# A decoder block in split fp32: VectorE and ScalarE keep the traced order from the big sets on, and the operands of w_down's parts are made at other places

## Chip, cores, metric

The kernel runs on one core of a Trainium2 chip. The metric is the device time of one execution in microseconds. Before the change it is 2761.99 us, the median of 3 runs (2760.24 to 2762.66).

## The reference

One decoder block over 512 tokens, model width 2048, in float32: two token mixers (latent attention and a gated DeltaNet) merged by gates, then a SwiGLU channel mixer of width 5632. The change lies in the channel mixer:

```python
h = _rmsnorm(x, norm_ffn[l]) * (1.0 + sc_f) + sh_f
gate, up = jnp.split(h @ w_gate_up[l], 2, axis=-1)
x = x + gt_f * ((jax.nn.silu(gate) * up) @ w_down[l])
...
return _rmsnorm(x, final_norm)
```

## The kernel before

**Split products.** Every float32 operand is split into a high part (a cast on ScalarE) and a low part (a subtraction on VectorE), and a product is three matmuls: high by high, low by high, high by low. Weights are read from HBM by loads on SP into tiles named `raw` or `raws`, split into `hi` and `lo`, and used by TensorE; four buffers hold each of `hi` and `lo`. Activations are kept as pairs too (`hilo`, L239 the cast and L240 the subtraction). All helpers of TensorE are recorded at L155.

**The driver.** The kernel's work is a list of units (L47 to L115). A unit has a load, a split, matmuls, and code before and after them. `fill` keeps `deep` units split ahead of the one that runs, and `ahead` more loaded (`LOADS`, or 2 where a unit sets it). While matmuls are traced, every `GROUP` = 12 of them the driver makes one `pump`: each side chain (a generator) goes one step further. `yield n` lets a chain rest for n pumps. So the Python code fixes a traced order: which evictions, splits and side steps stand between which matmuls.

**What sets the order on an engine.** `Core` wraps the engines in `PINNED`, before the change SP, GpSimd and TensorE, with `Ordered`: their instructions are carried out in the traced order. VectorE and ScalarE were not wrapped: there the tile layer's scheduler chose an order of its own.

**The channel mixer's stages.** `gu0` and `gu_both(1)` make the first columns of gate and up. `big(s)`, s = 1 to 10, makes 512 columns of each as a Strassen-like set of 7 products: 16 units, the first eight with 24 matmuls of 512 columns, the last eight with 18. `sums` (L1701) makes sums of weight blocks, `split` (L1722, L1723) their halves; the eviction code `after` (L1740 and on) combines the products from PSUM with VectorE, some with ScalarE, and `activated` multiplies silu(gate) by up later. The activations go to DRAM (`f_dram`), or stay as `aT`.

Then w_down. `dn(36, n)`, four plain sets of 2 units with 24 matmuls each; `strassen_down(0, n)`, n = 0 to 3, Strassen-like sets over 2048 rows of w_down; `dn(40, n)`; `strassen_down(1, n)`, whose last set runs in `last_dn` with the closing norm. A set of `strassen_down` has 8 units of 42 matmuls of 256 columns. Each unit's split has three sums (L1889), two casts (L1897) and two subtractions (L1898), of 768 and 1024 columns. The last unit of a set evicts: a copy of the first product (L1916, ScalarE), then seven sums on VectorE (L1913). Outputs are scaled on ScalarE (L1857) and added to DRAM by GpSimd.

**The operands of `strassen_down`.** `sums_down(ks)` is a side chain that makes the activations' combinations for q = 0 to 3; units 2q and 2q + 1 of each set use those of q. For each q it loads four blocks `a11`, `a21`, `a22`, `a12` from `f_dram` (`fetch_a`), makes four combinations (L1998) and splits seven operands with `hilo`, in four pumps of 3, 3, 3 and 2 VectorE instructions. `free(q)` says from when q may be made; it counts the operands of the earlier half that are done with (`gone`). While q is made, the next q's loads can be started step by step through `next(fetching, None)`. `down_ready` forces the remaining steps if a unit needs an operand that is not made yet. `dn` and `last_dn` use `wlh`, splits of w_down and of weights in another form, also by `hilo`.

Of the kernel before, what the change touches and what calls it, by code (L numbers as in the profile page):

```python
# [34 lines left out]
class Unit:  # L35


    def __init__(self, load=None, split=None, mms=None, pre=None, post=None, weight=1, alone=False, late=False):
        self.load = load
        self.split = split  # L40
        self.mms = mms
        self.pre = pre
        self.post = post
        self.weight = weight
        self.alone = alone
        self.late = late
# [97 lines left out]
class Ordered:  # L144


    def __init__(self, tc, engine):
        self.tc = tc
        self.engine = engine

    def __getattr__(self, name):
        f = getattr(self.engine, name)

        def call(*args, **kwargs):
            return self.tc.keep_in_program_order(f(*args, **kwargs))  # L155

        return call


class Core:  # L160
    def __init__(self, tc, pinned):
        nc = tc.nc
        for e in ("tensor", "vector", "scalar", "gpsimd", "sync"):
            setattr(self, e, Ordered(tc, getattr(nc, e)) if e in pinned else getattr(nc, e))

# [4 lines left out]
def block_kernel(ctx: ExitStack, tc: tile.TileContext, a: dict, out, out_t):  # L172
    nc = Core(tc, PINNED)
    drv = Driver()
# [372 lines left out]
    def logits_done(first):  # L547
        def done(ps):
            for j, q in enumerate(ps):
# [6 lines left out]
                        ks=[(k, 1) for k in range(KT)])  # L556
# [900 lines left out]
    def with_pre(units, fn):  # L1457
        u = units[0]
        p0 = u.pre

        def pre():
            fn()
            if p0 is not None:
                p0()
        u.pre = pre
        return units
# [177 lines left out]
    def combine():  # L1644

        for q in range(4):
            while h2n[1] < 2 * q + 10:
                yield
            a11, a12, a21, a22 = h2f[0][q], h2f[0][q + 4], h2f[1][q], h2f[1][q + 4]
            res = {}  # L1650
            for name, x, y, op in (("x5", a22, a21, ALU.subtract), ("x6", a11, "x5", ALU.add), ("x7", a11, a21, ALU.subtract),
                                   ("x3", "x6", a12, ALU.subtract)):
                x, y = (res.get(v, v) if isinstance(v, str) else v for v in (x, y))
                s = res[name] = S(name)
                nc.vector.tensor_tensor(s[:], x[:], y[:], op)
            comb[q] = {}
            for name in ("x3", "x6", "x7", "x5"):
                comb[q][name] = hilo(res.pop(name)[:], name)
                yield 2
            for h in range(2):  # L1660
                h2f[h][q] = h2f[h][q + 4] = None
            xn[0] = q + 1
# [304 lines left out]
    def sums_down(ks):  # L1967

        ahead = []

        def free(q):
            return q < 4 and gone[ks] >= min(q + 2, 4) and (q < 3 or plain_sets[0] > 4 * ks + 3)

        def fetch_a(q):
            v = {}
            for name, i, h in (("a11", 8 * ks + q, 0), ("a21", 8 * ks + q, 1), ("a22", 8 * ks + 4 + q, 1), ("a12", 8 * ks + 4 + q, 0)):
                v[name] = S(name)
                load(v[name][:], f_dram[i, h])
                yield 2
            ahead.append(v)  # L1980

        for q in range(4):
            if not ahead:
                yield from until(lambda: free(q))
                yield from fetch_a(q)
                yield 5
            v = ahead.pop(0)
            more = free(q + 1)
            if more:
                fetching = fetch_a(q + 1)  # L1990
            v["x7"] = S("x7")
            d = {}
            for c, dst, x, y, op in (("m7", "x7", "a11", "a21", ALU.subtract), ("m1", "a11", None, None, None),
                                     ("m5", "a21", "a22", "a21", ALU.subtract), ("m4", "a22", None, None, None),
                                     ("m6", "a11", "a11", "a21", ALU.add), ("m2", "a12", None, None, None),
                                     ("m3", "a12", "a11", "a12", ALU.subtract)):
                if op is not None:
                    nc.vector.tensor_tensor(v[dst][:], v[x][:], v[y][:], op)  # L1998
                d[c] = hilo(v[dst][:], "x")
                if op is None:  # L2000
                    if more and next(fetching, None) is None:
                        more = False
                    yield
            v = None
            if more:
                yield from fetching
            down[ks][q] = d
            made[ks] = q + 1
            yield
# [24 lines left out]
    def gu_both(s):  # L2034

        st = {}

        def unit(k0):
            box = {}

            def start():
                box["raw"] = fetch(gu_loads(s)(k0, 2), 512, 2)

            def split():
                box["w"] = halves(box.pop("raw"), 512, 2)

            def pre():
                if k0 == 0:
                    st["ps"] = [PS(f"gu{s}") for _ in range(4)]
                    st["done"] = gu_done(s, st["ps"])  # L2050

            def after(j, h):
                st["done"](j, h)

            mms = []
            for kk in range(2):
                k = k0 + kk
                for j in range(4):
                    for h in range(2):
                        for n, (wi, xi) in enumerate(((0, 0), (0, 1), (1, 0))):  # L2060
                            mms.append(lambda kk=kk, k=k, j=j, h=h, n=n, wi=wi, xi=xi: mm(
                                st["ps"][j][:, 256 * h:256 * h + 256], box["w"][wi][:, kk, tok(j)], half_k(h2T[h][k // 2], k)[xi],
                                start=k == 0 and h == 0 and n == 0, stop=k == KT - 1 and n == 2, skip_group_check=True))
                        if k == KT - 1:
                            mms[-1] = lambda m=mms[-1], j=j, h=h: (m(), after(j, h))

            def post():
                if k0 + 2 == KT:
                    for q in range(4):
                        h2T[1][q] = None  # L2070

            return Unit(start, split, mms, pre, post, late=k0 + 2 == KT)

        return [unit(k0) for k0 in range(0, KT, 2)]
# [15 lines left out]
    xc = []  # L2090

    def ffn():
        def gu0():
            us, st = [], {}

            def done(ps):
                done_ = gu_done(0, ps)
                for j in range(4):
                    for h in range(2):
                        done_(j, h)  # L2100

            for h in range(2):
                half = fm_set("gu0", gu_loads(0), 512, KT, lambda k, h=h: half_k(h2T[h][k // 2], k), done if h else None, st=st,
                              cols=slice(256 * h, 256 * h + 256), alone=True)
                for i, u in enumerate(half):
                    def ahead(h=h, k=min(2 * i + 4, KT)):
                        while h2n[h] < k:
                            drv.step(h2c[h])
                    with_pre([u], ahead)
                us.append(half)  # L2110

            def start():
                for j in range(KT):
                    mixT[j] = None
                start_h2(1)()
            with_pre(us[0], start)
            return us[0] + us[1]
# [171 lines left out]
        def finished(segs):  # L2289
# [3 lines left out]
            for q in range(8):  # L2293
# [3 lines left out]
                if q % 2:  # L2297
                    yield

        yield from gu0()  # L2300
        yield from with_pre(gu_both(1), lambda: xc.append(drv.add(combine())))
        assert known == {4, 5}
        side(g_dram.rearrange("(k p) -> p k", p=P), gt_ffn[:])
        nc.vector.tensor_scalar(gt_neg[:], gt_ffn[:], -1.0, None, op0=ALU.mult)
        euvw.append(wides.tile([P, 4, 512], F32, tag="wide", name="euvw"))
        for s in range(1, 11):
            for i, u in enumerate(big(s)):
                if (s, i) == (10, 10):
                    with_pre([u], lambda: maker.__setitem__(0, drv.add(sums_down(0))))
                yield u  # L2310

# [1 line left out]
            drv.ahead = LOADS  # L2313
        for n in range(4):
            for k, u in enumerate(dn(36, n)):
                yield with_pre([u], more)[0]
                if n in (1, 2):
                    yield Unit(mms=turned_a(2 * n + k - 2), pre=lambda: drv.finish(chains["act"]))
        for n in range(4):
# [7 lines left out]
                yield u  # L2327
        for n in range(4):
            for u in dn(40, n):
                yield with_pre([u], more)[0]  # L2330
        for n in range(3):
            yield from strassen_down(1, n)
        yield from last_dn()
# [62 lines left out]
```

## Time and profile before

| | us |
|---|---|
| median of 3 runs | 2761.99 |
| the profiled execution | 2757.97 |
| its span in the trace | 2755.9 |
| of it, the big sets | 1484.20 to 2264.36 |
| `dn(36)` | 2264.36 to 2309.80 |
| `strassen_down(0, 0)` begins | 2309.64 |
| `strassen_down(1, 0)` begins | 2527.07 |

A page of the profile gives busy time by engine; PE is TensorE, DVE VectorE, ACT ScalarE, POOL GpSimd, SP the engine that issues most loads. Because TensorE is almost always busy, its few idle places matter, and its granted clock, which is 1.00 at full speed. In a list of waits, "PE m <- DVE xl" is idle time of TensorE before a matmul into m that ended when VectorE had written xl.

### The profile page before, as it was taken

The numbers are of one execution on the slowest core, as the hardware profiler recorded it, in microseconds if no ns is written. First come the engines' busy times: TensorE is split into PE (matmuls) and PEld (weight loads), VectorE is DVE, ScalarE is ACT, GpSimd is POOL, SyncE is SP. The second block draws the span as 40 slices with busy tenths as digits, with TensorE's granted clock in tenths as the row PEclk, the third lists the DMA queues.
The fourth block names the chain that finished last, engine by engine and source line by source line (L and its number), as shares of the span: only waits on it lengthen the run. The fifth ranks groups of instructions, "written<-read, shape, count | busy, mean of one in ns | idle before, by whom it ended". The sixth has DMA issues, their size and how long they took to land.

```text
span 2755.9 us, 39855 instructions
## 1 busy us (share of the span) xinstructions
PE 2726.4 (99%) x14896; PEld 2348.2 (85%) x14896; DVE 2017.6 (73%) x3193; ACT 1168.9 (42%) x1649; POOL 251.5 (9%) x334
## 2 busy tenths in 40 slices
PE   9999999999999999999999999999999999999998
PEld 7888788888888888888999888888888888998997
DVE  8884657676967547785487877778877867878876
ACT  3443432542344343222373444444444445446545
POOL 0000011102100000001000000000000103113113
PEclk9999999999999999999999999999999999999999
DMA  9996556546754648885464565666565668469565
GB/s 350 313 364 203 152 162 179 190 146 182 211 150 153 203 143 287 306 298 195 158 182 146 189 202 199 207 213 201 200 210 191 213 204 193 115 194 207 123 190 173
DMA packets 308538, 557.93 MB, mean 202 GB/s; under 512 B 39956, under 2 KB 109748, under 8 KB 308216
## 3 DMA queue, kind: packets, MB, share of 16 engines
q1 hardware_dynamic: 259848, 461.09, 51.6%
q0 software_dynamic: 28704, 66.37, 9.3%
q10 hardware_dynamic: 19792, 27.92, 2.9%
q8 instruction: 116, 1.90, 0.3%
q14 instruction: 78, 0.64, 0.1%
HBM read 474.52 MB, written 80.76 MB: 201 GB/s over the span
## 4 chain that ended last, share of the span: by engine, by line
PE 94%; DVE 2%; DMA 2%; issue 1%; ACT 1%; SPq 0%; ACTq 0%; DVEq 0%; POOLq 0%
PE m L155 37%; PE wo L155 6%; PE gb L155 6%; PE v L155 4%; PE gu L155 3%; PE z L155 3%; PE ga L155 3%; PE ya L155 3%; PE k L155 3%; PE dn L155 3%; PE q L155 3%; PE yb L155 3%; PE s L155 3%; PE ckv L155 2%; PE cq L155 2%; PE qk L155 1%
## 5 line engine op out<-in xcount | busy, mean ns | idle before, releaser
L263 ACT CAST hi<-raw 128x1024 fp32r<-128x1024 f32 (+1 forms) x274 | 285.2, 1042 | 666.7 <-DMA raw<-in_w_in_dram 131.2
L264 DVE TENSOR_TENSOR lo<-raw,hi 128x1024 fp32r<-128x1024 f32 (+1 forms) x274 | 337.2, 1232 | 305.4 <-ACT hi L263 291.8
L1722 ACT CAST hi<-raws 128x512 fp32r<-128x512 f32 (+1 forms) x240 | 218.4, 910 | 329.0 <-PE m L155 270.4
L1723 DVE TENSOR_TENSOR lo<-raws,hi 128x512 fp32r<-128x512 f32 (+1 forms) x240 | 247.7, 1044 | 86.5 <-ACT hi L1722 86.3
L155 PE MATMUL m<-xl,hi 128*128 128x256 f32 x896 | 257.1, 287 | 3.8 <-DVE xl L240 3.8
L155 PE MATMUL m<-xh,hi 128*128 128x256 f32 x896 | 256.8, 287 | 3.7 <-ACT xh L239 2.3
L155 PE MATMUL m<-xh,lo 128*128 128x256 f32 x896 | 256.6, 286 | 0.8 <-DVE lo L1898 0.8
L435 DVE CUSTOM_DVE_ANT_0 rawm<-rawm,cbc 128x1024 f32<-128x1024 f32 x192 | 234.1, 1238 | 7.8 <-DMA rawm<-in_w_mod_dram 7.2
L155 PE MATMUL m<-hi,h2h 128*128 128x512 f32 x480 | 190.7, 397 | 0.4 <-DVE euvw L1740 0.3
L155 PE MATMUL m<-hi,h2l 128*128 128x512 f32 x480 | 187.2, 390 | 0.0
L155 PE MATMUL m<-lo,h2h 128*128 128x512 f32 x480 | 186.8, 389 | 0.0
L155 PEld LDWEIGHTS m<-xl,hi 128*128 128x128 f32 x896 | 175.0, 195 | 4.7 <-DVE xl L240 4.7
L155 PEld LDWEIGHTS m<-xh,hi 128*128 128x128 f32 x896 | 175.0, 195 | 4.4 <-ACT xh L239 2.7
L155 PEld LDWEIGHTS m<-xh,lo 128*128 128x128 f32 x896 | 175.2, 196 | 1.0 <-DVE lo L1898 1.0
L1722 ACT CAST hi<-sums 128x1024 fp32r<-128x1024 f32 x80 | 84.2, 1052 | 109.2 <-PE m L155 104.2
L1723 DVE TENSOR_TENSOR lo<-sums,hi 128x1024 fp32r<-128x1024 f32 x80 | 97.8, 1222 | 27.3 <-ACT hi L1722 26.8
L155 PE MATMUL wo<-mh,hi 128*128 128x512 f32 (+1 forms) x320 | 111.2, 347 | 0.0
L155 PE MATMUL wo<-mh,lo 128*128 128x512 f32 (+1 forms) x320 | 110.9, 347 | 0.0
L155 PE MATMUL wo<-ml,hi 128*128 128x512 f32 (+1 forms) x320 | 110.9, 347 | 0.0
L1897 ACT CAST hi<-sums 128x1024 fp32r<-128x1024 f32 x64 | 67.1, 1048 | 99.0 <-PE m L155 76.7
L1898 DVE TENSOR_TENSOR lo<-sums,hi 128x1024 fp32r<-128x1024 f32 x64 | 78.2, 1223 | 39.8 <-ACT hi L1897 39.6
L155 PEld LDWEIGHTS m<-hi,h2l 128*128 128x128 f32 x480 | 90.1, 188 | 19.5
(535 smaller groups left out, 7315.9 us busy)
## 6 DMA issues: line engine op xcount, KB each, us to landing
raws<-in_w_gate_up_dram SPq DMA_DIRECT2D x400, 256.0 KB, 3.5
rawm<-in_w_mod_dram SPq DMA_DIRECT2D x192, 512.0 KB, 5.5
raw<-in_w_in_dram SPq DMA_DIRECT2D x144, 512.0 KB, 4.7
raws<-in_w_down_dram SPq DMA_DIRECT2D x128, 256.0 KB, 4.1
raw<-in_w_o_dram SPq DMA_DIRECT2D x40, 512.0 KB, 4.6
s_dram<-raws POOLq DMA_DIRECT2D x80, 256.0 KB, 2.3
raws<-s_dram SPq DMA_DIRECT2D x80, 256.0 KB, 3.3
rawa<-in_w_in_dram SPq DMA_DIRECT2D x32, 512.0 KB, 4.4
```

The lines of the kernel that those rows point to most:

```text
L155: return self.tc.keep_in_program_order(f(*args, **kwargs))
L263: nc.scalar.copy(hi[:], raw[:])
L264: (lo_eng or nc.vector).tensor_tensor(lo[:], raw[:], hi[:].bitcast(F32), ALU.subtract)
L435: r = nc.vector.tensor_tensor_reduce(raw, raw, c, 1.0, 0.0, ALU.mult, ALU.add, parts[:, k, half:half + 1])
L1722: nc.scalar.copy(hi[:], src)
L1723: nc.vector.tensor_tensor(lo[:], src, hi[:].bitcast(F32), ALU.subtract)
L1897: nc.scalar.copy(hi[:], src)
L1898: nc.vector.tensor_tensor(lo[:], src, hi[:].bitcast(F32), ALU.subtract)
```

## The change

From the first of the big sets on, VectorE and ScalarE keep the traced order too: all five engines are wrapped, and `on` of those two is set there. `free` gets lower thresholds, `fetch_a` and the pause after it yield fewer pumps, and `sums_down(0)` starts two units earlier. The loads go two units ahead rather than four from unit 3 of `gu_both(1)` on and from the third set of each `dn`.

```diff
@@ class Ordered
-    def __init__(self, tc, engine):
+    def __init__(self, tc, engine, on=True):
         self.tc = tc
         self.engine = engine
+        self.on = on
...
-            return self.tc.keep_in_program_order(f(*args, **kwargs))
+            ins = f(*args, **kwargs)
+            return self.tc.keep_in_program_order(ins) if self.on else ins
@@ class Core
-            setattr(self, e, Ordered(tc, getattr(nc, e)) if e in pinned else getattr(nc, e))
+            setattr(self, e, Ordered(tc, getattr(nc, e), e in pinned))
@@ def sums_down(ks)
-            return q < 4 and gone[ks] >= min(q + 2, 4) and (q < 3 or plain_sets[0] > 4 * ks + 3)
+            return q < 4 and gone[ks] >= (0 if ks == 0 else 2, 2, 3, 4)[q] and (q < 3 or plain_sets[0] > 4 * ks + 3)
...
                 load(v[name][:], f_dram[i, h])
-                yield 2
+                yield
...
                 yield from fetch_a(q)
-                yield 5
+                yield 3
@@ the channel mixer
+        def few():
+            drv.ahead = 2
+
         yield from gu0()
-        yield from with_pre(gu_both(1), lambda: xc.append(drv.add(combine())))
+        us = with_pre(gu_both(1), lambda: xc.append(drv.add(combine())))
+        with_pre([us[3]], few)
+        yield from us
...
+        nc.vector.on = nc.scalar.on = True
         for s in range(1, 11):
             for i, u in enumerate(big(s)):
-                if (s, i) == (10, 10):
+                if (s, i) == (10, 8):
                     with_pre([u], lambda: maker.__setitem__(0, drv.add(sums_down(0))))
                 yield u
...
             for k, u in enumerate(dn(36, n)):
-                yield with_pre([u], more)[0]
+                yield with_pre([u], more if n < 2 else few)[0]
...
             for u in dn(40, n):
-                yield with_pre([u], more)[0]
+                yield with_pre([u], more if n < 2 else few)[0]
```

Traced this way, the first loads and steps of q land at other places: q0 of half 0 is made in units 12 to 15 of the tenth big set (before, in `dn(36)`), q1 in `dn(36)` (before, at the start of the first `strassen_down` set), q0 of half 1 in unit 6 of `strassen_down(0, 3)` (before, in `dn(40)`). The order of TensorE's and GpSimd's instructions is the same in both kernels. SP issues 38 loads from `f_dram` in place of 32.

## The prediction

> **What bounds the kernel now.** First the page:
>
> ```profile
> span 2755.9 us, 39855 instructions
> PE 2726.4 (99%) x14896; PEld 2348.2 (85%) x14896; DVE 2017.6 (73%) x3193; ACT 1168.9 (42%) x1649; POOL 251.5 (9%) x334
> ```
>
> TensorE works 99% of the span. The change removes no instruction from it, so it can gain only where TensorE waits or runs at a lower clock. Where that is, the table of windows shows (window, its length, then busy time and instructions of PE, weight loads, DVE, ACT and POOL, granted clock, DMA share, GB/s):
>
> ```profile
> 1484.20:2264.36 780.16, 779.80 (x3508) 644.95 (x3507) 609.00 (x701) 349.82 (x417) 62.82 (x116) 1.00 0.61 202
> 2264.36:2309.80 45.44, 45.44 (x211) 37.60 (x210) 28.26 (x41) 24.15 (x38) 20.34 (x21) 1.00 0.93 207
> 2309.80:2353.75 43.95, 37.88 (x277) 36.59 (x276) 40.62 (x65) 23.78 (x35) 3.87 (x4) 0.89 0.57 157
> 2485.30:2530.00 44.70, 44.70 (x210) 37.50 (x210) 32.46 (x48) 30.57 (x49) 20.48 (x19) 1.00 1.05 226
> 2530.00:2573.00 43.00, 43.00 (x360) 43.00 (x360) 41.65 (x66) 24.02 (x35) 3.87 (x6) 1.00 0.52 126
> 2661.00:2705.00 44.00, 41.83 (x334) 41.41 (x333) 28.81 (x46) 21.50 (x39) 8.97 (x14) 0.96 0.74 232
> ```
>
> In order: the big sets (0.36 us idle in 780), `dn(36)` (none), `strassen_down(0,0)` (6.07 us idle, clock 0.89), `dn(40)` (none), `strassen_down(1,0)` (none, though VectorE is busy 41.65 of 43) and `strassen_down(1,3)` (2.17 us idle). The waits of TensorE from 1400 on (us, times, longest) name the same places:
>
> ```profile
> PE m L155 <- DVE xl L240: 3.8, 4, 1.2
> PE m L155 <- ACT xh L239: 2.3, 2, 1.1
> PE m L155 <- ACT hi L1897: 1.4, 1, 1.4
> PE m L155 <- DVE lo L1898: 0.8, 1, 0.8
> PE m L155 <- DVE euvw L1740: 0.3, 1, 0.3
> ```
>
> The first two are the operands that `sums_down` makes, late in `strassen_down(0,0)`; the next two are the weight split in `strassen_down(1,3)`. An idle stretch also costs clock behind it, as 5-us windows around the stretches show:
>
> ```profile
> 2330.00:2335.00 5.00, 2.23 (x13) 1.53 (x11) 5.00 (x9) 1.92 (x3) 0.00 (x0) 0.85 0.07 25
> 2335.00:2340.00 5.00, 4.48 (x21) 4.48 (x22) 4.40 (x9) 2.39 (x4) 0.00 (x0) 0.50 0.31 102
> 2350.00:2355.00 5.00, 4.04 (x18) 3.84 (x19) 4.11 (x8) 0.83 (x1) 0.00 (x0) 0.56 0.29 90
> 2355.00:2360.00 5.00, 5.00 (x35) 5.00 (x34) 1.25 (x2) 1.73 (x3) 0.00 (x0) 0.76 0.36 105
> 2675.00:2680.00 5.00, 2.83 (x16) 2.42 (x15) 4.26 (x6) 2.71 (x4) 0.00 (x0) 0.83 0.58 193
> 2680.00:2685.00 5.00, 5.00 (x37) 5.00 (x37) 4.08 (x7) 3.78 (x5) 0.00 (x0) 0.83 0.52 163
> ```
>
> After some 3 us idle the next 4.04 + 5.00 us of matmuls lose 0.44 x 4.04 + 0.24 x 5.00 = 3.0 us; after 2.17 us idle 0.17 x (2.83 + 5.00) = 1.3 us. I price a stall with its clock so. What each set loses in all, the evicting copy of its first product tells (ScalarE's timeline: start, length), against the matmul with which the set begins (TensorE's timeline):
>
> ```profile
> 2309.41 0.39 PE L155 MATMUL dn<-ah,lo 128*128 128x512 f32 x1
> 2309.64 0.28 PE L155 MATMUL m<-xh,hi 128*128 128x256 f32 x1
> ...
> 2527.07 0.28 PE L155 MATMUL m<-xh,hi 128*128 128x256 f32 x1
> ```
>
> ```profile
> 2358.62 0.58 ACT L1916 COPY euvw<-m 128x512 f32<-128x512 f32 x1
> 2398.92 0.58 ACT L1916 COPY euvw<-m 128x512 f32<-128x512 f32 x1
> 2563.42 0.58 ACT L1916 COPY euvw<-m 128x512 f32<-128x512 f32 x1
> 2644.06 0.58 ACT L1916 COPY euvw<-m 128x512 f32<-128x512 f32 x1
> 2688.46 0.59 ACT L1916 COPY euvw<-m 128x512 f32<-128x512 f32 x1 [4.01 <-PE m L155]
> ```
>
> A steady set is 2398.92 - 2358.62 = 40.3 us: 8 units of 5.04 us, each 42 matmuls of 0.12. From the set's first matmul to the copy, set (0,0) took 48.98 us and set (1,0) 36.35: (0,0) lost 12.6 us, (1,0) nothing. Set (1,3) took 44.40: it lost 4.1. So 16.7 us are to be had; everything else is cover that can be lost.
>
> **The change part by part.** The durations, from VectorE's timeline (the start of each to the next is its cost in a row):
>
> ```profile
> 2330.30 0.69 DVE L240 TENSOR_TENSOR xl<-a,xh 128x512 fp32r<-128x512 f32 x1
> 2330.90 0.42 DVE L1889 TENSOR_TENSOR sums<-sums,raws 128x256 f32<-128x256 f32 x1
> 2331.24 0.69 DVE L240 TENSOR_TENSOR xl<-a,xh 128x512 fp32r<-128x512 f32 x1
> ...
> 2332.78 0.95 DVE L1898 TENSOR_TENSOR lo<-raws,hi 128x768 fp32r<-128x768 f32 x1
> 2333.64 1.22 DVE L1898 TENSOR_TENSOR lo<-sums,hi 128x1024 fp32r<-128x1024 f32 x1
> 2334.78 0.69 DVE L240 TENSOR_TENSOR xl<-a,xh 128x512 fp32r<-128x512 f32 x1
> ```
>
> and ScalarE's around set (1,3)'s wait:
>
> ```profile
> 2674.88 1.14 ACT L239 CAST wlh<-raw 128x512 fp32r<-128x512 f32 x2 [8.62 <-DMA raw<-in_w_down_dram]
> 2675.93 1.04 ACT L1897 CAST hi<-sums 128x1024 fp32r<-128x1024 f32 x1
> ```
>
> VectorE takes 0.60 us for 512 columns, 0.34 for 256, 0.86 for 768, 1.14 for 1024; two `wlh` casts in 1.14 make an `xh` cast some 0.6.
>
> One q of `sums_down` is 11 VectorE instructions, 6.6 us if nothing waits. Kept in order, each of its first three pumps is a sum (0.69), the cast (0.6), and two differences (0.60 each), 2.5 us, the last 1.9: **9.4 us**. Before, other splits filled those round trips and q's rows stood wherever the scheduler put them; now a q stays behind whatever the code traced ahead of it. In that order every q in a Strassen-like set has its pumps two to four, or all four, behind the `lo` of a unit's split, whose buffer is free only when TensorE ends the unit two before it.
>
> The loads (KB each, us from issue to landing):
>
> ```profile
> raws<-in_w_down_dram SPq DMA_DIRECT2D x128, 256.0 KB, 4.1
> ...
> a<-f_dram SPq DMA_DIRECT2D x32, 256.0 KB, 5.1
> ```
>
> The thresholds in `free` and the shorter yields act only through these places. `few` has two weight units under way instead of four, 10 us of matmuls against loads of 4.1: 0; cover gone, it would show as waits for `raws`.
>
> *Pinning in the big sets.* 0. TensorE lacks 0.36 us there, of which a gain of 0.3 is possible. At a set's change six 0.60-us evictions and a split (0.60 + 0.60 + 1.14) stand in one row, 5.94 us, against a unit of 24 or 18 matmuls, 5.48 or 4.11 us at the 0.23 from the `dn` matmul above to the next; splits are one unit early, which covers it. Cover gone, it is 1.83 us a set, 18 over the ten sets: the upper bound.
>
> *`few` and two units earlier for q0 of half 0; set 10 into `dn(36)`.* +4. q0's pumps now start at unit 12 of set 10. Pumps two to four follow a 1024-wide `lo` whose cast waits for unit 13's end, 28 matmuls or 6.4 us after the first pump is traced; then cast and `lo` 2.2, two pumps 5.0, the first `lo` of `dn(36)` 1.1, the last pump 1.9: 16.6 us, where set 10's last matmul is done at 64 x 0.23 = 14.6. The evictions that free `dn(36)`'s banks, and its second `lo`, stand behind: 2 x 0.60 for the first bank, 1.14 more for each `lo`. TensorE stalls 1.5 us at the first group and 1.2 at the second operand, with clock 1.3. Lower bound 0 (its copies go out on ScalarE first), upper 7.
>
> *Set (0,0).* -1. q0 and q1 are done before it, so its first four units run. q2 goes behind the `lo` that waits for unit 1's end: cast 1.05, `lo` 1.22, three pumps 2.5 + 2.5 + 1.9, then unit 4's sums 0.60 + 2 x 0.34 and `lo` 0.86, 11.3 us against units 2 and 3, 10.1: 1.3 us, up to 2.4 with the second `lo`; I take 2, and 1.3 of clock. q3 stands wholly behind the `lo` of unit 6's split, which waits for unit 4's end: 2.3 + 9.4 = 11.7 us, while unit 5 takes 5.04. Unit 6 needs the third pump for its second product and the fourth for its third, so it stalls 5.2 to 6.7; I take 5.5, and 3.0 of clock. That is 11.8 us lost, where 12.6 were. Bounds -7 (only q3's stall, without clock) to +6 (the upper values, and loads that are late by the 5.1 us in which they land).
>
> *`dn(40)`.* +5. q0 of half 1 is now traced in unit 6 of set (0,3), behind a `lo` that waits for unit 6's 18th matmul: 2.3 + 9.4 = 11.7 us, against 69 matmuls of 0.12 to `dn(40)`'s second group, 8.3. The first product's copy (ScalarE) and all seven evictions (VectorE) are behind q0: 3.4 us of stall and some 1.6 of clock. Bounds 0 (the row of `dn(40)` shows no idle time now) and 6.4.
>
> *Set (1,0).* +12. q2 and q3 stand as in set (0,0): 2 + 1.3 + 5.5 + 3.0 = 11.8, and nothing was lost before. Bounds +5 (q3's stall alone) and +18 (the upper values and late loads).
>
> *Set (1,3).* -4. ScalarE waited 8.62 us in a `wlh` cast with a split's cast behind; the traced order puts the split's cast ahead. Bounds -4.1 and 0.
>
> *`fetch_a`.* 0. A plain `yield` gives None, which the caller reads as the end: only one load of the next q goes out, six are wasted (each a turn on SP's queue ahead of weight loads, and a slot, which the lead of two units hides), and a q's loads start when the q before is done, 50 to 80 matmuls ahead (6 to 10 us against 5.1). Cover gone, 5 us a q. The closing part after the last set keeps its order of matmuls: 0, give or take 1.
>
> Sum: 0 + 4 - 1 + 5 + 12 - 4 = +16 on the profiled execution's 2757.97; the median of the runs shown stands 4.0 above that, so 2761.99 + 16 = **2778 us**.
>
> On the clock a page speaks against my terms: the Trainium skill, "TensorE: Matmul & The Clock Gate", section "Why this matters for your kernels", has the clock fall only after gaps above about 3 us. The rows disagree: 2.17 us idle, and 0.83 behind it.
>
> **The rivals.**
> *Faster:* the earlier q1 takes 6.6 us off VectorE's 40.62 in set (0,0); if the stalls of q2 and q3 then are short in both first sets, 12.6 + 4.1 come back: 2745. For it: those two waits are all that TensorE has. Against it: q3's order behind unit 4's end. It decides if unit 6 of set (0,0) waits under 1 us.
> *No change:* set (1,0) loses what (0,0) and (1,3) regain, the `dn` stalls are covered by banks already free: 2762.
> *Slower by much:* splits at the big sets' changes come late by more than the unit of lead, 1.83 us in each of ten: 2778 + 18 = 2796. Against it: VectorE is busy 609 of 780 us there. For it: evictions now hold the row.
> *Short stalls cost no clock* (the page's rule above would do this): the clock terms of the stalls under 3 us fall out, 1.3 in `dn(36)`, 1.3 in each first set: 2778 - 4 = 2774. The row at 2675 speaks against it.
>
> **How the numbers follow.** The forecast has 0.48, short stalls without clock 0.06, much slower 0.18, no change 0.11, faster 0.17. Range 2752 to 2802: it leaves out most of the fast case and the upper bounds all together; the likeliest case's own is 2764 to 2794. A difference under 0.2% (5.5 us) can't be told from none. Faster 0.17, within 0.11, slower 0.72.
>
> **What would show it.** Right: idle TensorE after 1484 falls into four places, unit 6 of set (0,0) and of (1,0) with waits for `xl` of 4 to 7 us, the first groups of `dn(36)` and `dn(40)`, waiting for evictions or `lo`; in set (1,3) no wait for `hi`; `f_dram` loads 38 rather than 32. Wrong: a copy less than 40 us after the start in set (0,0) (then q's order costs nothing), more than 5 us idle in the big sets, or set (1,0) still at 36.4 us.

## The result and the profile after

The changed kernel takes 2799.97 us (median of 4 runs, 2795.62 to 2801.07), the kernel before 2761.69 on the same chip: a ratio of 1.0136, 95% interval 1.0119 to 1.0154. It is slower, as forecast, but by 38 us in place of 16. The page of the changed kernel's profiled execution (2795.62 us) begins:

```profile
span 2793.9 us, 39911 instructions
...
PE 2738.7 (98%) x14896; PEld 2352.3 (84%) x14896; DVE 2026.5 (73%) x3193; ACT 1160.1 (42%) x1649; POOL 251.3 (9%) x334
```

Every engine has as many instructions as before (the 56 more of the total are none that count as busy), and the span is longer by 38.0 us. The waits of TensorE from 1400 on (us, times, longest), in which all engines now show L156, the line of the wrapper; `euvw` and `g` are written by evictions, `hss` belongs to the closing norm:

```profile
PE m L156 <- ACT xh L156: 7.0, 2, 3.5
PE dn L156 <- ACT hi L156: 5.7, 3, 3.1
PE m L156 <- DVE lo L156: 4.8, 3, 1.9
PE dn L156 <- ACT euvw L156: 3.3, 1, 3.3
PE m L156 <- ACT hi L156: 2.6, 2, 1.3
PE dn L156 <- DVE lo L156: 1.1, 2, 0.5
PE hss L156 <- DVE sq L156: 0.9, 1, 0.9
PE m L156 <- DVE xl L156: 0.8, 3, 0.3
PE dn L156 <- ACT g L156: 0.5, 1, 0.5
```

Waits before `dn` matmuls were not there before. The table of windows, cut at the stages of this run (window, length, busy time of PE, weight loads, DVE, ACT and POOL, granted clock, DMA share, GB/s):

```profile
2268.44:2324.50 56.06, 49.97 (x208) 39.23 (x208) 29.89 (x41) 26.73 (x40) 20.14 (x21) 0.94 0.84 183
2324.50:2374.20 49.70, 42.68 (x305) 41.20 (x304) 39.70 (x58) 22.63 (x32) 4.06 (x4) 0.86 0.51 123
...
2546.90:2595.70 48.80, 41.45 (x302) 39.62 (x301) 38.19 (x56) 23.11 (x32) 4.86 (x4) 0.90 0.50 121
2595.70:2676.30 80.60, 80.60 (x673) 80.59 (x673) 67.27 (x97) 36.52 (x50) 7.06 (x8) 1.00 0.53 136
...
2774.30:2793.90 19.60, 0.01 (x1) 0.00 (x0) 9.65 (x25) 6.89 (x14) 0.40 (x1) 0.58 0.36 134
```

The rows are `dn(36)`, set (0,0), set (1,0), sets (1,1) and (1,2), and what follows the last matmul. Both first sets now lose alike. In `dn(36)`'s window, which begins just behind its first wait (1.28 us), TensorE is idle for 6.09 us at a clock of 0.94. From the last matmul's start (2773.93) to the end it takes 19.9 us, against 12.7 before (from 2743.26).

Since TensorE's order is the same in every run here, the n-th matmul of one trace can be set against the n-th of another. How much later (us) a stage's last matmul starts than in the profile of before, less the same at the stage's beginning, is what the stage lost; "tail" is from the last matmul to the end. The runs below use the same measure; before the big sets the runs differ by 0.1 to 4.6 us, which is left out, as are the sets between the first and the last of each half (at most 0.5 us but for 4.33 in (0,1) to (0,3) of e6):

| | big sets | dn(36) | (0,0) | dn(40) | (1,0) | (1,3) | closing matmuls | tail |
|---|---|---|---|---|---|---|---|---|
| forecast | 0 | +4 | -1 | +5 | +12 | -4 | 0 | 0 |
| after | 1.75 | 12.36 | 0.59 | 5.38 | 12.33 | -2.63 | 0.04 | 7.25 |
| e1 asks only | -0.19 | 0.00 | -6.54 | 0.80 | 6.04 | -0.02 | 0.00 | -0.40 |
| e2 order, old asks | 1.77 | 9.30 | 7.39 | 2.81 | 14.09 | -2.85 | 1.62 | 6.63 |
| e3 tail given back | 1.76 | 13.64 | 0.71 | 6.21 | 13.49 | -1.94 | 0.15 | 0.12 |
| e4 order in big sets only | 1.85 | 3.21 | -6.78 | 1.39 | 3.40 | -1.01 | -0.09 | -0.39 |
| e5 VectorE only | 1.85 | 7.27 | 0.89 | 6.56 | 12.05 | -4.24 | 2.64 | 6.69 |
| e6 ScalarE only | 0.69 | 4.93 | -6.45 | 0.95 | 7.34 | -1.85 | 5.01 | -0.38 |
| e7 q1 late | 1.75 | 9.50 | 24.13 | 5.21 | 13.63 | -2.28 | 1.65 | 7.13 |
| e8 asks, prefetch mended | 0.87 | 0.39 | -12.61 | 1.07 | 0.00 | 0.10 | 0.03 | 0.00 |
| e9 after, prefetch mended | 1.75 | 19.05 | -8.74 | 13.01 | 3.89 | -1.93 | 1.65 | 6.33 |
| e10 after, fill first | 1.79 | 6.01 | 1.03 | 5.39 | 12.25 | -2.70 | 1.69 | 7.25 |
| e11 e8, order in (1,3) | 2.77 | 0.35 | -12.61 | 1.91 | 0.00 | -4.24 | 1.78 | 0.01 |

Four terms hold to within 2 us: (0,0), `dn(40)`, (1,0) and (1,3). `dn(36)` (+8.4 over the forecast) and the tail (+7.3) carry most of what was missed, the big sets 1.75.

One execution's value carries some scatter. Ahead of the last matmul the traces grant a clock of 1.00 or 0.5, and the stretches at 0.5 last 3.41 us or a multiple of it, so one more or less is 1.7 us (3.41 x 0.5). The 1.6 to 1.8 of the closing matmuls in e2, e7, e9, e10 and e11 is mainly one such stretch (in e2, 0.50 from 2755.31 to 2758.72, behind a wait of 0.87 us; behind one as long the changed kernel keeps 1.00).

### The profile page after: what moved, and what is told of

Same layout as the page of the kernel before. It is cut to its first block, busy times and chain, and to the rows that moved or that the text cites. A ratio compares the mean times of both kernels' runs of the same rounds, so it can differ in the third digit from the quotient of the medians.

```text
span 2793.9 us, 39911 instructions
## 1 busy us (share of the span) xinstructions
PE 2738.7 (98%) x14896; PEld 2352.3 (84%) x14896; DVE 2026.5 (73%) x3193; ACT 1160.1 (42%) x1649; POOL 251.3 (9%) x334
## 4 chain that ended last, share of the span: by engine, by line
PE 88%; DVE 5%; ACT 2%; DMA 2%; issue 2%; POOL 0%; SPq 0%; ACTq 0%; DVEq 0%; POOLq 0%
PE m L156 36%; PE wo L156 6%; PE gb L156 6%; PE v L156 4%; PE gu L156 3%; PE z L156 3%; PE ya L156 3%; PE k L156 3%; PE q L156 3%; PE yb L156 3%; PE s L156 3%; PE dn L156 3%; PE ckv L156 2%; PE cq L156 2%; PE qk L156 1%
## 5 line engine op out<-in xcount | busy, mean ns | idle before, releaser
L156 DVE TENSOR_TENSOR lo<-raw,hi 128x1024 fp32r<-128x1024 f32 (+1 forms) x274 | 337.0, 1232 | 314.2 <-ACT hi L156 300.6
L156 ACT CAST hi<-raw 128x1024 fp32r<-128x1024 f32 (+1 forms) x274 | 284.6, 1042 | 648.2 <-DMA raw<-in_w_in_dram 128.6
L156 ACT CAST hi<-raws 128x1024 fp32r<-128x1024 f32 (+2 forms) x304 | 269.2, 892 | 385.6 <-PE m L156 236.9
L156 DVE TENSOR_TENSOR lo<-raws,hi 128x1024 fp32r<-128x1024 f32 (+2 forms) x304 | 311.4, 1024 | 160.3 <-ACT hi L156 160.3
L156 PE MATMUL m<-xh,hi 128*128 128x256 f32 x896 | 258.1, 288 | 9.6 <-ACT xh L156 7.0
L156 PE MATMUL m<-xh,lo 128*128 128x256 f32 x896 | 257.4, 287 | 4.8 <-DVE lo L156 4.8
L156 PE MATMUL m<-xl,hi 128*128 128x256 f32 x896 | 257.7, 288 | 1.1 <-DVE xl L156 0.8
L156 ACT CAST hi<-sums 128x1024 fp32r<-128x1024 f32 x144 | 151.2, 1050 | 216.8 <-PE m L156 117.3
L156 DVE CUSTOM_DVE_ANT_0 rawm<-rawm,cbc 128x1024 f32<-128x1024 f32 x192 | 234.1, 1238 | 8.6 <-DMA rawm<-in_w_mod_dram 8.4
L156 DVE TENSOR_TENSOR lo<-sums,hi 128x1024 fp32r<-128x1024 f32 x144 | 176.0, 1222 | 50.9 <-ACT hi L156 50.9
L156 PE MATMUL m<-hi,h2h 128*128 128x512 f32 x480 | 190.5, 397 | 0.0
L156 PE MATMUL m<-lo,h2h 128*128 128x512 f32 x480 | 188.0, 392 | 0.1
L156 PE MATMUL m<-hi,h2l 128*128 128x512 f32 x480 | 187.4, 390 | 0.0
L156 PEld LDWEIGHTS m<-xh,hi 128*128 128x128 f32 x896 | 175.6, 196 | 11.2 <-ACT xh L156 7.9
L156 PEld LDWEIGHTS m<-xh,lo 128*128 128x128 f32 x896 | 175.6, 196 | 5.5 <-DVE lo L156 5.4
L156 PEld LDWEIGHTS m<-xl,hi 128*128 128x128 f32 x896 | 175.4, 196 | 2.5 <-DVE xl L156 2.4
L156 PE MATMUL wo<-mh,hi 128*128 128x512 f32 (+1 forms) x320 | 111.3, 348 | 0.0
L156 PE MATMUL wo<-mh,lo 128*128 128x512 f32 (+1 forms) x320 | 111.0, 347 | 0.0
L156 PE MATMUL wo<-ml,hi 128*128 128x512 f32 (+1 forms) x320 | 111.0, 347 | 0.0
L156 PEld LDWEIGHTS m<-lo,h2h 128*128 128x128 f32 x480 | 90.3, 188 | 21.3 <-DVE lo L156 3.9
L156 PEld LDWEIGHTS m<-hi,h2l 128*128 128x128 f32 x480 | 90.1, 188 | 19.0
L156 PEld LDWEIGHTS m<-hi,h2h 128*128 128x128 f32 x480 | 90.2, 188 | 17.4
```

Of the source, the lines that this page charges most:

```text
L156: ins = f(*args, **kwargs)
```

## The experiments

**The order or the requests (e1, e2).** e1 is the change without the line that keeps VectorE and ScalarE in order:

```diff
-        nc.vector.on = nc.scalar.on = True
```

> All of the change except that VectorE and ScalarE stay with the scheduler's order. If the loss comes from keeping the order, no stage after 2264 us loses: 2755 to 2765 us, and set (0,0), whose q0 and q1 are asked for earlier, may gain up to 12 us (down to 2750). If the loss comes from the earlier requests themselves (more loads, fewer weights under way, slots), it stays at 2780 or above.

Measured 2759.18 us, ratio 0.9998 (0.9988 to 1.0007): no difference from before. Set (0,0) gained 6.5 us, which the order theory allowed; that (1,0) lost 6.0 it did not foresee. Of these waits from 1400 on, half stand in each of the two sets, where before all stood in (0,0):

```profile
PE m L156 <- DVE xl L156: 2.7, 4, 0.7
PE m L156 <- ACT xh L156: 2.5, 2, 1.3
```

e2 is the other half: the order kept and `few`, the rest as before.

```diff
-            return q < 4 and gone[ks] >= (0 if ks == 0 else 2, 2, 3, 4)[q] and (q < 3 or plain_sets[0] > 4 * ks + 3)
+            return q < 4 and gone[ks] >= min(q + 2, 4) and (q < 3 or plain_sets[0] > 4 * ks + 3)
...
-                yield
+                yield 2
-                yield 3
+                yield 5
-                if (s, i) == (10, 8):
+                if (s, i) == (10, 10):
```

> The order kept and `few`, but `free`, both yields and q0's start as before the change. Order theory: the big sets (+3.5) and the part after the last set (+7.4) lose as with the whole change, and q3 of half 1, asked for 21 matmuls before it is needed, stalls set (1,0) by 7 us and more: 2790 to 2810. Rival, that the earlier requests do the harm in dn(36), dn(40) and set (1,0) (28 us of the 38): 2770 to 2775.

Measured 2802.14 us, ratio 1.0153 (1.0138 to 1.0168), as expected. Keeping the order costs as much without the earlier requests as with them; the requests choose where. So `dn(36)`'s first wait, which comes with q0's earlier start, is not there in e2, while its waits at the later changes of set are.

**The tail (e3).** In the whole change, both engines go back to the scheduler's order when the first unit after `strassen_down(1,3)` begins:

```diff
+        def pinned(on):
+            nc.vector.on = nc.scalar.on = on
...
                 if q == 0:
                     with_pre([u], lambda: drv.finish(chains["act"]))
+                    with_pre([u], lambda: pinned(False))
```

> The whole change, with the two engines given back to the scheduler from the first unit after strassen_down(1,3) on. If the last 7.4 us are the four-step chains of the closing norm standing in a row, 7 to 8 us come back: 2792 us, and from the last matmul to the end about 12 us as before. If they come from something earlier that ends late, it stays at 2800.

Measured 2793.34 us, ratio 1.0122 (1.0105 to 1.0139): the tail's 7.25 us fell to 0.12. How they arise is read on VectorE's timeline of the changed kernel after the last matmul (start, length, what; in brackets idle time ahead and what ended it):

```profile
2773.93 0.69 DVE L156 TENSOR_TENSOR x2t<-x2t,dn 128x512 f32<-128x512 f32 x1
2775.47 0.69 DVE L156 TENSOR_TENSOR x2t<-x2t,row 128x512 f32<-128x512 f32 x1 [0.85 <-ACT dn L156]
2776.08 0.68 DVE L156 TENSOR_TENSOR dn<-dnt,row 128x512 f32<-128x512 f32 x1
2776.80 0.69 DVE L156 TENSOR_TENSOR x2t<-x2t,dn 128x512 f32<-128x512 f32 x1
2778.34 0.69 DVE L156 TENSOR_TENSOR x2t<-x2t,row 128x512 f32<-128x512 f32 x1 [0.85 <-ACT dn L156]
```

Each of the last token tiles is a product, a sum, a square on ScalarE, and a product over the sum's own tile. In a row, the next tile's first product waits behind the square: one tile every 2.87 us (2775.47 to 2778.34), its matmuls done before. So VectorE is some tiles behind TensorE: the last sum starts 8.60 us after the last matmul (2782.53), where it was 1.78 before (2745.04). Before the change, the scheduler had put the next tile's rows and those of the norm's root into that wait, here on the same engine:

```profile
2743.69 0.69 DVE L2240 TENSOR_TENSOR dn<-dnt,row 128x512 f32<-128x512 f32 x1 [0.20 <-PE dnt L155]
2744.30 0.15 DVE L232 SCALAR_TENSOR_TENSOR rs<-rs,rs 128x1 f32<-128x1 f32 x1
2744.36 0.68 DVE L2243 TENSOR_TENSOR x2t<-x2t,row 128x512 f32<-128x512 f32 x1
...
2745.04 0.68 DVE L2241 TENSOR_TENSOR x2t<-x2t,dn 128x512 f32<-128x512 f32 x1
```

**Order in the big sets alone (e4).** The engines go back to the scheduler at the first unit of `dn(36)`, by the same function:

```diff
             for k, u in enumerate(dn(36, n)):
+                if (n, k) == (0, 0):
+                    with_pre([u], lambda: pinned(False))
```

> The whole change, with the two engines given back to the scheduler at dn(36)'s first unit. The big sets' slow drift (+3.5 us by 2264) stays, and what q0 in the tenth set does to the first groups of dn(36) (+2 to 3); all else is gone: 2766 to 2769 us. If the later losses hang on the requests and not on the order, 2780 and more.

Measured 2762.36 us, ratio 1.0012 (1.0003 to 1.0022), some 4 us under what was expected, because (0,0) gains here as in e1 by more than (1,0) loses. The big sets' loss of 1.85 us stays. In every run with VectorE in order there (after, e2 to e5, e7, e9, e10) it is the same step at nine changes of set: in the new set's second unit the first product by `lo` starts 0.40 us after the one ahead, where 0.23 is steady, and the next 0.33. TensorE's timeline of the changed kernel at the first change:

```profile
1566.50 0.39 PE L156 MATMUL m<-hi,x5l 128*128 128x512 f32 x1
1566.72 0.39 PE L156 MATMUL m<-hi,h2h 128*128 128x512 f32 x1
1567.12 0.50 PE L156 MATMUL m<-lo,h2h 128*128 128x512 f32 x1
1567.45 0.40 PE L156 MATMUL m<-hi,h2l 128*128 128x512 f32 x1
```

That is 0.28 us a change, 2.5 us over nine, less some 0.9 of waits that before had and this has not: the rival "slower by much" is there, at 0.28 a change and not 1.83. The runs without VectorE's order there (e1, e6, e8, e11) have no such step; their values in this column are a few single waits, of up to 1.7 us.

**Which engine's row (e5, e6).** The whole change with only one engine in order:

```diff
-        nc.vector.on = nc.scalar.on = True
+        nc.vector.on = True
```

> The whole change with only VectorE kept in order, ScalarE with the scheduler. If VectorE's row carries the stalls of q2 and q3 and the closing part, sets (0,0) and (1,0) and the last 7 us look as with the whole change, and only dn(36), whose stalls stand behind y copies on ScalarE, recovers most of its 12 us: about 2785 to 2790. If ScalarE's row is what matters, 2765 to 2770.

Measured 2795.13 us, ratio 1.0125 (1.0107 to 1.0142), 5 us above what was expected. VectorE alone brings (0,0), (1,0) and the tail to the values of the whole change. `dn(36)` still lost 7.3 us, which was not expected: TensorE waited 3.08 us for its first `lo`, 0.55 for `g`, and 1.33 for one later `lo`.

```diff
-        nc.vector.on = nc.scalar.on = True
+        nc.scalar.on = True
```

> The whole change with only ScalarE kept in order. The complement of the run before: dn(36) still loses 8 to 12 us, the sets (1,0) and the closing part lose little: 2770 to 2778. If both rows are needed for a stall, 2762.

Measured 2773.8 us, ratio 1.0047 (1.0031 to 1.0063), inside what was expected, but the parts differ: `dn(36)` 4.9 where 8 to 12 were expected, (1,0) only 1.3 more than e1, 4.3 in (0,1) to (0,3) (one wait of 2.60 us for `lo`, and clock), and 5.0 in the closing matmuls, which neither the whole change nor VectorE's row alone shows to that size. In `dn(36)` the two runs part what the whole change has: e5 has the wait at the first operands, and e6 has none there, but 1.55 + 0.52 and 1.27 + 0.52 us at two later changes of set, the first of them behind four copies.

**`dn(36)` (e7, e10).** Its stalls in the changed kernel are 2.36 us at the first groups, near the 2.7 worked out, and two more at changes of set, 3.22 and 1.79, that the forecast lacked. The first stall is three waits: 1.28 for the first operand's cast, 0.53 for its `lo`, and 0.55 for `g`. ScalarE's timeline around the larger:

```profile
2288.86 0.62 ACT L156 CAST xh<-x 128x512 fp32r<-128x512 f32 x1 [1.36 <-DVE x L156]
2289.38 0.62 ACT L156 CAST xh<-a 128x512 fp32r<-128x512 f32 x1
2291.44 1.14 ACT L156 CAST xh<-a 128x512 fp32r<-128x512 f32 x2 [1.44 <-DVE a L156]
2292.48 2.41 ACT L156 ACTIVATE y<-dn,gt_ffn 128x512 f32<-128x512 f32 x4
2294.77 1.06 ACT L156 CAST hi<-raw 128x1024 fp32r<-128x1024 f32 x1
```

Two pumps of q1, then the four copies `y` of the set that ended, 2.41 us, and only then the cast of the next weight, for which TensorE waits until 2295.88. `dn`'s units are `late`: their next split is traced after their matmuls and evictions. e7 takes q1 out of there, e10 the copies:

```diff
-            return q < 4 and gone[ks] >= (0 if ks == 0 else 2, 2, 3, 4)[q] and (q < 3 or plain_sets[0] > 4 * ks + 3)
+            return q < 4 and gone[ks] >= (0 if ks == 0 else 2, 2, 3, 4)[q] and (q < (1 if ks == 0 else 3) or plain_sets[0] > 4 * ks + 3)
```

> The whole change, order kept, but q1 of half 0 only made once dn(36) is through. If dn(36)'s second and third stall (3.2 and 1.8 us, with clock some 8 of its 12 us) are q1's pumps and four y copies standing ahead of the next weight cast on ScalarE, dn(36) loses 4 to 5 us in place of 12; q1 then stalls unit 2 of set (0,0) by 3 to 6 us. If they come from `few` or from late loads, dn(36) stays at 12.

Measured 2819.96 us, ratio 1.0217 (1.0198 to 1.0237). The larger stall shrank from 3.22 to 1.79, but no further: `dn(36)` lost 9.5, not 4 to 5. And q1, traced in set (0,0), delayed every q behind it, so that the set lost 24 us where 3 to 6 were expected for unit 2:

```profile
PE m L156 <- ACT xh L156: 21.7, 6, 4.8
PE m L156 <- DVE xl L156: 1.4, 6, 0.2
```

```diff
-            if u.post is not None:
-                u.post()
             if u.late:
                 self.fill()
+            if u.post is not None:
+                u.post()
```

> The whole change, order kept, but after a `late` unit the next split is traced ahead of the evictions (fill before post). If dn(36)'s stalls of 1.27 + 0.52 us at each change of set are four y copies (4 x 0.60 us) ahead of the next weight cast on ScalarE, they go in dn(36): 4 to 8 us less there, 2790 to 2796. If they come from the loads, nothing changes. The split's cast then stands ahead of the copies that free PSUM banks, which could cost the same elsewhere.

Measured 2792.61 us, ratio 1.0117 (1.0103 to 1.0131): `dn(36)` lost 6.0 in place of 12.4, and no other stage moved by more than 1.7. The stall at the later change is gone whole. ScalarE's timeline at the same place:

```profile
2292.61 1.14 ACT L156 CAST xh<-a 128x512 fp32r<-128x512 f32 x2 [1.44 <-DVE a L156]
2293.66 1.04 ACT L156 CAST hi<-raw 128x1024 fp32r<-128x1024 f32 x1
2294.60 1.84 ACT L156 ACTIVATE y<-dn,gt_ffn 128x512 f32<-128x512 f32 x3
```

The cast now follows the pumps at once, and its stall is 0.79 + 0.53 us. So the copies traced ahead of the cast made some 1.8 us at each of these two changes of set, q1's pumps another 1.4 at one of them.

**The dropped prefetch (e8, e9).** `next(fetching, None) is None` can't tell a plain `yield` from the end. With another mark the loads of the next q go out while a q is made (32 loads in place of 38):

```diff
-                    if more and next(fetching, None) is None:
+                    if more and next(fetching, 0) == 0:
```

e8 is e1, the scheduler's order, with this.

> The earlier requests with the scheduler's order, with next() told apart from its end, so that a q's loads start while the q before is made: 32 loads from f_dram. If set (1,0)'s loss of 6.0 us without pinning comes from loads that start only when q2 is done, it goes, and set (0,0)'s gain of 6.5 stays: 2751 to 2756. If q3 is late because of where it is asked for, 2759 as without this.

Measured 2752.04 us, ratio 0.9974 (0.9964 to 0.9983): faster than before. Its waits of TensorE from 1400 on hold no operand of `sums_down` any more (no `xh`, no `xl`):

```profile
PE m L156 <- ACT hi L156: 1.6, 1, 1.6
PE m L156 <- DVE euvw L156: 1.5, 1, 1.5
PE m L156 <- DVE lo L156: 0.8, 1, 0.8
```

Set (0,0) regained all of its 12.6 us, and (1,0) loses nothing. e9 is the whole change with the same edit.

> The whole change, order kept, with next() told apart from its end as in the run before. If the stalls of q2 and q3 under the kept order come from q's place behind a split that waits for TensorE, loads that start earlier change nothing: sets (0,0) and (1,0) keep their 3.2 + 3.9 us, 2797 to 2801. If they come from late loads, both sets clear as they did with the scheduler's order: 2770 to 2776.

Measured 2796.79 us, ratio 1.0127 (1.0114 to 1.0141). The time is within 0.3 us of what was expected, the reason is not: the stalls for q3 did go, in both sets. Waits came back elsewhere, as the waits from 2260 to 2600 show:

```profile
PE dn L156 <- ACT hi L156: 5.2, 5, 1.3
PE aT L156 <- DVE g L156: 4.9, 1, 4.9
PE dn L156 <- DVE lo L156: 4.6, 7, 1.4
...
PE dn L156 <- ACT euvw L156: 3.4, 1, 3.4
```

Against the whole change, (0,0) gained 9.3 us and (1,0) 8.4, `dn(36)` lost 6.7 more and `dn(40)` 7.6: the q's are now traced among the plain sets, and stand ahead of their splits there.

e9 moves both q3's loads and its place, so it can't tell the two apart. The changed kernel's own timelines of ScalarE and VectorE can, here in set (0,0):

```profile
2355.95 1.05 ACT L156 CAST hi<-sums 128x1024 fp32r<-128x1024 f32 x1 [2.53 <-PE m L156]
2357.02 1.23 DVE L156 TENSOR_TENSOR lo<-sums,hi 128x1024 fp32r<-128x1024 f32 x1 [0.69 <-ACT hi L156]
2358.17 0.69 DVE L156 TENSOR_TENSOR x<-a,a 128x512 f32<-128x512 f32 x1
```

Unit 6's cast waits until unit 4 has ended (unit 5's first matmul starts at 2355.82), its `lo` follows, and q3's first sum stands right behind. In (1,0) that sum starts at 2581.20, while q3's four loads had landed by 2570.55. So in the whole change the place holds q3 back, not the loads.

**Order where it helps (e11).** e8 with both engines in order only from the first unit of `strassen_down(1,3)` to its end, by the function `pinned` of e3.

> The earlier requests with the working prefetch and the scheduler's order, and the two engines kept in order only in strassen_down(1,3). There the whole change gained 3.5 us: 2.3 us of stall at 2670 to 2672 and its clock should go, 2748 to 2750 against 2752 without; if the gain needs the rows before it in order too, 2752.

Measured 2748.26 us (5 runs, 2744.67 to 2752.51), ratio 0.9953 (0.9939 to 0.9966), the fastest seen: set (1,3) gained 4.24 us, all that it had lost, where e8 gained nothing. The intervals of the ratios of e8 and e11 still overlap a little, so that this gain rests on the trace, in which TensorE works through the set (window, length, busy times, clock as above):

```profile
2641.30:2682.00 40.70, 40.70 (x341) 40.70 (x340) 31.09 (x44) 19.35 (x29) 11.10 (x18) 1.00 0.79 240
```

## Why the prediction was right in sign and wrong in size

Two steps of the sum failed. The term of `dn(36)` was mis-sized: +4 was worked out and 12.36 us came, because the working stopped at the first operands. The term of the closing part was put at 0 from the order of the matmuls alone, and 7.25 us came behind the last of them. Together they are 15.6 of the 22 us that the sum lacked.

- *`dn(36)`, +4:* mis-sized. The first stall was 2.36 us for 2.7, and e2, with q0's old start, doesn't have it; but its first wait ended with the weight's cast and not with an eviction. Left out was that later sets there have four copies ahead of the next cast on ScalarE, and q1 ahead of those: 5.0 us more of stall. With clock it is 12.36 in all, outside its bound of 7. e10 shows the copies, e7 q1's smaller part.
- *The closing part, 0, "give or take 1":* wrong. It was argued from the order of the matmuls, which says nothing of a chain between VectorE and ScalarE behind them. 7.25 us, undone by e3.
- *Set (1,0), +12:* right in place and in what holds the row; the size is in part luck. TensorE waited 1.30 + 1.88 us in unit 4, where 2, at most 2.4, was worked out, and 3.5 + 0.5 in unit 6, where 5.5, at least 5.2, was; the two errors cancel. It waited 7.35 in all, and clock makes up the rest (0.90 in its window). Unit 6's wait was mostly for `xh`, not for `xl`. *Set (0,0)*, -1 against 0.59: the same two stalls, and the same luck. The rows behind `lo` are VectorE's (e5 has them, e6 mostly not).
- *`dn(40)`, +5:* right. The second group waited 3.33 us for the first product's copy, 3.4 in the working.
- *Big sets, 0, bound 18:* 1.75. The lead of a unit covers a change of set but for 0.28 us. The rival "slower by much" gave 2796, near the 2800 measured, but what it names makes only 1.75 us of the 38.
- *Set (1,3), -4:* 2.63 in the whole change, which still waits 1.07 us for a `lo` in the set's last unit; e11 has all 4.24. The reason given was ScalarE's order, but e5, with only VectorE in order, gains 4.24 too, and e6, with only ScalarE, 1.85.
- *What is to be had, and what is cover:* right. Unpinned and with its prefetch, the earlier asking regains (0,0)'s 12.6 us (e8), and order in (1,3) the rest (e11): the rival "faster" was possible, but not with the order kept.
- *`fetch_a`, 0:* right only as a load count. That the prefetch is dropped decides where in the traced order q2 and q3 stand, and so in which stage the stalls fall (e9), and with the scheduler's order it costs the 6 us in each first set (e1 against e8).
- *Clock:* in the window behind unit 4's stall the granted clock was 0.52, then 0.80. Behind `dn(36)`'s first stall, three waits with matmuls between, it stayed at 1.00 in the changed kernel and in e4, so the 1.3 us of clock worked out for it did not come. In e10 that stall was only 1.27 + 0.52 us, and the clock was 0.50 for the next 3.41 us. A flat price per idle time was too simple. The Trainium skill ("TensorE: Matmul & The Clock Gate", section "Why this matters for your kernels", no gaps above about 3 us) fits e4; it does not fit the 0.50 in e10, the 0.52 here or the 0.83 after set (1,3)'s 2.17 us before the change.

The 5-us windows of the changed kernel around unit 4's stall, then two windows of e4 around and behind its first `dn(36)` stall:

```profile
2342.00:2347.00 5.00, 3.34 (x26) 2.93 (x24) 3.57 (x6) 2.50 (x4) 0.00 (x0) 1.00 0.43 160
2347.00:2352.00 5.00, 3.48 (x16) 3.48 (x17) 4.58 (x8) 2.14 (x3) 0.00 (x0) 0.52 0.36 104
2352.00:2357.00 5.00, 5.00 (x36) 5.00 (x36) 3.94 (x6) 2.46 (x3) 0.00 (x0) 0.80 0.35 106
```

```profile
2267.00:2271.00 4.00, 2.20 (x8) 1.00 (x7) 3.12 (x4) 2.11 (x4) 0.00 (x0) 1.00 0.25 95
2271.00:2275.00 4.00, 3.44 (x15) 2.74 (x15) 3.79 (x6) 4.00 (x8) 0.00 (x0) 1.00 0.59 196
```

What stays open: what in ScalarE's row alone made TensorE wait in the closing matmuls. In e6 it waited there 0.86 + 1.68 us for `wll`, the low part of a `wlh` split, and the granted clock was 0.50 for 6.83 us; no run takes this apart. Nor does one show why the whole change gains less in set (1,3) than e5 and e11.

## What to carry to other kernels

An order that is kept must be priced on every stretch in which it holds, the tail behind the last matmul too, and engine by engine: list what each helper engine has in its row between the moment a buffer comes free and the moment its result is needed. Where the traced order puts evictions ahead of the next operand's split, keep the scheduler's order or trace the split first. Keep an order only in the stage where a wait is queued ahead of work that is ready (here one set, 4.2 us), and test a generator's end by a mark that it can't yield.

## What the runs showed of the hardware that was not expected

The granted clock fell behind several short waits, none of them over 2 us, and it was not decided by their sum. Behind `dn(36)`'s first stall it was 0.50 for 3.41 us in e10 (1.27 + 0.52 us idle), and stayed at 1.00 in e4 (1.27 + 0.53 + 0.56) and in the changed kernel (1.28 + 0.53 + 0.55). Two waits of 1.30 and 1.88 us, 0.5 us apart, were followed by 0.52 and 0.80 in the next two 5-us windows. Why the same matmuls keep the clock in one execution and not in another is not shown.
